# A softmax kernel: one scaled row in eight on ScalarE, and the last four rows of two tiles loaded in DMAs of chosen partition counts

## The chip, the cores and the metric

The kernel runs on one core of a Trainium2 chip. The metric is the device time of one execution in microseconds (us). HBM is the large memory that holds x and the result, SBUF the memory beside the engines, with 128 partitions (rows). A DMA is a transfer between the two; 16 DMA engines carry it out in packets, and each engine ends its part with a semaphore write of 4 bytes, which marks its data as landed (before the change the packet records hold 160 for the ten loads and 128 for the eight stores, 16 each). The median before the change is 162.49 us (2 runs, 162.41 to 162.57). Apart from one experiment, which is marked, all runs were in the fast state. Times "in the span" count from the start of the profiled span, which is about 1.8 us shorter than the device time.

## The reference

```python
x = randn(16, 1024, 512)            # float32, 32 MiB
x_scaled = x / 0.5
exp_x = exp(x_scaled - max(x_scaled, axis=-1))
out = exp_x / sum(exp_x, axis=-1)   # float32, 32 MiB
```

This is a softmax over rows of 512. Every byte is read once and written once: 33.55 MB in, 33.55 MB out.

## The kernel before

The 16,384 rows form eight tiles of 128 partitions x 16 rows x 512 elements (4 MiB, 32 KiB in each partition, contiguous in HBM). SP issues the loads, ACT (ScalarE) the stores. VectorE (DVE) finds the maxima, ScalarE does the exponentials with their sums. The scaling by 1/sum is divided: VectorE takes three rows in four, ScalarE one in four. The kernel keeps six tiles in SBUF, so load 6 must wait for store 0 and load 7 for store 1.

```python
LOADS = [[(0, 1), (1, 4), (4, G)]] + [WHOLE] * 7          # G = 16 rows
BLOCKS = [[(0, 4), (4, 8), (8, G)]] + [WHOLE] * 6 + [[(0, 8), (8, G)]]
...
def load(c):
    ...
    for lo, hi in LOADS[c]:
        nc.sync.dma_start(out=xt[:, lo:hi, :], in_=xr[c][:, lo:hi, :])
...
def scale_vector(i):
    ...
    k = b - b // 4
    ...                              # DVE: rows 0..k of the block times recip
def scale_scalar(i):
    for g in range(b - b // 4, b):
        ...                          # ACT: one copy with a scale per row
...
for i in range(n):
    if i + 1 < n:
        exponentials(i + 1)
    scale_vector(i)
    scale_scalar(i)
    if i + 2 < n:
        shift(i + 2)                 # loads its tile, then maxima on DVE
    store(i)
```

## Time and profile before

| | before |
|---|---|
| device time, median | 162.49 us |
| DVE busy, ACT busy | 125.6 us (78%), 112.5 us (70%) |
| DMA engines: the two data queues, share of the 16 engines' span | 49.3% + 48.4% |
| one 32 KiB packet, load or store (packet records of the trace) | 1.213 us, so 27.0 GB/s per engine |
| last store issued | 140.3 us |
| store 6 landed on the 16 engines | 148.6 to 149.5 us |
| last store landed | 158.3 to 159.2 us |

The first lines are from the page of the kernel before: busy time by engine, then the span in 40 slices (each digit is the busy share in tenths) with the rate in GB/s, the two data queues (q1 carries the loads, q10 the stores), two groups (busy us, mean ns, idle time before them and its cause), and the issues of whole tiles with their median time to landing.

```profile
...
DVE 125.6 (78%) x45; ACT 112.5 (70%) x290; POOL 0.2 (0%) x4
...
DVE  0507999999999999999999999999799994800000
ACT  3071759089989989995999599959998969600000
...
DMA  5999999999999999999999999999999999999993
GB/s 169 477 398 465 449 392 465 449 392 443 465 392 392 400 392 498 416 392 473 441 394 457 449 400 441 465 400 432 473 400 416 481 400 416 489 400 408 498 400 139
...
q1 hardware_dynamic: 1440, 33.56, 49.3%
q10 hardware_dynamic: 1152, 33.55, 48.4%
q14 instruction: 3, 0.02, 0.0%
...
L74 DVE TENSOR_REDUCE negmax<-xt 128x16 f32<-128x8192 f32 (+2 forms) x11 | 69.9, 6353 | 10.7 <-DMA xt<-in_x_dram 10.7
L102 DVE TENSOR_TENSOR xt<-xt,recip 128x6144 f32<-128x6144 f32 (+2 forms) x11 | 52.9, 4813 | 0.4
...
out_dram<-xt ACTq DMA_DIRECT2D x8, 4096.0 KB, 24.8
xt<-in_x_dram SPq DMA_DIRECT2D x7, 4096.0 KB, 29.8
...
```

All DMA slices but the first and last read 9, and the two queues together fill 97.7% of the engines' span. VectorE also reads 9 in most slices from the fifth to the 33rd, but it has finished after slice 35, while DMA goes on to the end. The timeline of the kernel before shows the last store's issue (start, duration, engine):

```profile
...
140.32 0.34 ACTq L119 DMA_DIRECT2D out_dram<-xt  x1
```

At 140.3 us the engines still have 8 to 9 us of store 6 ahead of them, and then they need about 9.7 us for the last store (eight packets of 1.213 us each; store 7 lands 9.7 us after store 6 in the table). From an issue to its first packet some 1 us passes (0.73 to 1.72 us for the first load). Compute is therefore about 7 us early at the tail, and the kernel is bounded by the bytes of each DMA engine.

### The profile page before, as it was taken

What the parts mean: (1) busy time and instruction counts of PE and PEld (TensorE: products, weight loads), DVE (VectorE), ACT (ScalarE), POOL (GpSimd) and SP (SyncE); (2) the same over time, 40 slices, a digit from 0 to 9 for tenths busy, and PEclk for the clock granted to TensorE, in tenths of its full rate; (3) what the DMA queues carried; (4) which work ended last, traced back from release to release, by engine and by line L of the source; (5) the groups of instructions that cost most, each with busy time, mean ns of one, the idle gap of its engine ahead of it and who ended that gap; (6) DMA issues with size and microseconds to landing.
All of it is one profiled execution on the core that took longest, in us unless ns stands there. A gap on an engine that the chain in (4) does not pass through costs nothing.

```text
span 160.7 us, 421 instructions
## 1 busy us (share of the span) xinstructions
DVE 125.6 (78%) x45; ACT 112.5 (70%) x290; POOL 0.2 (0%) x4
## 2 busy tenths in 40 slices
DVE  0507999999999999999999999999799994800000
ACT  3071759089989989995999599959998969600000
POOL 0000000000000000000000000000000000000000
DMA  5999999999999999999999999999999999999993
GB/s 169 477 398 465 449 392 465 449 392 443 465 392 392 400 392 498 416 392 473 441 394 457 449 400 441 465 400 432 473 400 416 481 400 416 489 400 408 498 400 139
DMA packets 2595, 67.13 MB, mean 418 GB/s; under 512 B 289, under 2 KB 289, under 8 KB 545
## 3 DMA queue, kind: packets, MB, share of 16 engines
q1 hardware_dynamic: 1440, 33.56, 49.3%
q10 hardware_dynamic: 1152, 33.55, 48.4%
q14 instruction: 3, 0.02, 0.0%
HBM read 33.55 MB, written 33.55 MB: 418 GB/s over the span
## 4 chain that ended last, share of the span: by engine, by line
DMA 41%; DVE 24%; ACT 19%; issue 1%; SPq 1%; ACTq 0%
DMA xt<-in_x_dram 23%; DMA out_dram<-xt 18%; ACT xt L85 17%; DVE negmax L74 15%; DVE xt L102 8%; ACT xt L111 2%; DVE bias L78 1%; SPq L66 1%; DVE recip L100 0%; ACTq L119 0%; ACTq L85 0%
## 5 line engine op out<-in xcount | busy, mean ns | idle before, releaser
L85 ACT ACTIVATE xt<-xt,bias 128x512 f32<-128x512 f32 x128 | 90.4, 707 | 25.8 <-DVE bias L78 24.8
L74 DVE TENSOR_REDUCE negmax<-xt 128x16 f32<-128x8192 f32 (+2 forms) x11 | 69.9, 6353 | 10.7 <-DMA xt<-in_x_dram 10.7
L102 DVE TENSOR_TENSOR xt<-xt,recip 128x6144 f32<-128x6144 f32 (+2 forms) x11 | 52.9, 4813 | 0.4
L85 ACT ACTIVATION_READ_ACCUMULATOR xt<-xt,bias 128x1 f32 x128 | 23.9, 187 | 0.0
L111 ACT ACTIVATE xt<-xt,recip 128x512 f32<-128x512 f32 x32 | 20.5, 706 | 0.0
L100 DVE RECIPROCAL recip<-sums 128x16 f32<-128x16 f32 (+2 forms) x11 | 2.4, 218 | 2.3 <-ACT xt L85 2.3
L78 DVE TENSOR_SCALAR bias<-negmax 128x16 f32<-128x16 f32 (+2 forms) x11 | 1.9, 173 | 0.4
L52 ACT ACT_TABLE_LOAD x1 | 1.3, 1283 | 0.7 <-PEq L148 0.7
L51 DVE MEMSET warm<- 128x1 f32 x1 | 0.1, 59 | 0.8 <-PEq L148 0.8
L52 ACT ACTIVATE warm<-warm 128x1 f32<-128x1 f32 x1 | 0.2, 203 | 0.0
L148 POOL MEMSET const-bfloat16-1.0<- 128x1 bf16 x1 | 0.1, 102 | 0.0
L148 POOL MEMSET const-uint8-127<- 128x1 uint8 x1 | 0.1, 102 | 0.0
L148 POOL MEMSET const-float32-0.0<- 128x1 f32 x1 | 0.1, 99 | 0.2 <-issue 0.2
L148 POOL MEMSET const-float32-1.0<- 128x1 f32 x1 | 0.1, 99 | 0.0
## 6 DMA issues: line engine op xcount, KB each, us to landing
out_dram<-xt ACTq DMA_DIRECT2D x8, 4096.0 KB, 24.8
xt<-in_x_dram SPq DMA_DIRECT2D x7, 4096.0 KB, 29.8
xt<-in_x_dram SPq DMA_DIRECT2D x1, 3072.0 KB, 11.3
xt<-in_x_dram SPq DMA_DIRECT2D x1, 768.0 KB, 4.5
xt<-in_x_dram SPq DMA_DIRECT2D x1, 256.0 KB, 2.8
```

The lines of the kernel that those rows point to most:

```text
L51: nc.vector.memset(warm, 0.0)
L52: nc.scalar.activation(out=warm, in_=warm, func=EXP)
L66: nc.sync.dma_start(out=xt[:, lo:hi, :], in_=xr[c][:, lo:hi, :])
L74: nc.vector.tensor_reduce(negmax[:, 0:b], chunks[c][:, lo:hi, :], axis=AX, op=MAX, negate=True)
L78: nc.vector.tensor_scalar_mul(biases[i][:, 0:b], negmax[:, 0:b], 2.0)
L85: nc.scalar.activation(out=row, in_=row, func=EXP, bias=biases[i][:, g : g + 1], scale=2.0, accum_out=sums[i][:, g : g + 1],)
L100: nc.vector.reciprocal(recips[i][:, 0:b], sums[i][:, 0:b])
L102: nc.vector.tensor_mul(rows, rows, recips[i][:, 0:k].unsqueeze(2).broadcast_to((P, k, D)))
L111: nc.scalar.activation(out=row, in_=row, func=COPY, scale=recips[i][:, g : g + 1])
L148: nc = _bacc.Bacc("TRN2", target_bir_lowering=False, num_devices=1)
```

## The change

The intent is to move scaling work from ScalarE to VectorE, to simplify the first load, and to load the last four rows of tiles 1 and 2 in DMAs of 2, 6, 10, 14, 96 and 4, 8, 8, 12, 96 partitions. The counts were meant to give different DMA engines different numbers of packets, so that they can be told apart.

```diff
-    LOADS = [[(0, 1), (1, 4), (4, G)]] + [WHOLE] * 7
+    LOADS = [[(0, 4), (4, G)]] + [WHOLE] * 7
 ...
+        if c in SPLITS:
+            load_split(c)
+            return
 ...
+    SPLITS = {1: [2, 6, 10, 14, 96], 2: [4, 8, 8, 12, 96]}
+    LAST = slice(G - 4, G)
+
+    def load_split(c):
+        nc.sync.dma_start(
+            out=chunks[c][:, 0 : G - 4, :], in_=xr[c][:, 0 : G - 4, :]
+        )
+        p = 0
+        for k in SPLITS[c]:
+            nc.sync.dma_start(
+                out=chunks[c][p : p + k, LAST, :], in_=xr[c][p : p + k, LAST, :]
+            )
+            p += k
+        assert p == P
 ...
-        k = b - b // 4
+        k = b - b // 8
 ...
-        for g in range(b - b // 4, b):
+        for g in range(b - b // 8, b):
```

## The prediction

> **What bounds the kernel now: the 16 DMA engines, each by its own bytes.** The page's slices show DMA at 9 in 38 of 40 (queues: 49.3% + 48.4% of the engines' span). The packet records are sharper: a 32 KiB packet takes 1.213 us, load or store (27.0 GB/s per engine); packets sum to 156.8 us per engine, between the first at 1.72 us and the last landing at 159.2 us of a 160.7 us span. DVE is 78% busy, ACT 70%. The last store is issued at 140.3 us (timeline) but store 6 lands only at 148.6 to 149.5 us, so compute has about 7 us of slack at the tail.
>
> **What the change does**
>
> 1. Scale split. DVE multiplies 7/8 instead of 3/4 of the rows: 128x6144 takes 6.56 us, 128x3072 3.36 us, so 128x7168 about 7.65 and 128x3584 about 3.92 (estimates by line): +9.3 us over 11 blocks, about 135 us busy. ACT loses 16 copies of 0.706 us (112.5 to about 101). DVE is gapless from 13 to 114 us, so all shifts: the last tile's reductions start near 120.8 us instead of 114.9 (the 1.1 us wait for that load vanishes). The last store goes out near 148 us, not 140.3. This eats nearly all the slack, but hardly more: first packets can run at about 149.1 us (the first load took 1.0 us from issue to packet), against 148.6 to 149.5 us when the engines finished store 6 before.
>
> 2. First load in two DMAs instead of three. Tile 0 lands at about 12.4 us, while its 256 KiB per engine at 27.0 GB/s from 1.72 us would be 11.4. About 0.2 us may be regained.
>
> 3. Marked loads. [...] Before, the last store's landings spread from 158.3 to 158.8, with one engine at 159.2: an average engine plus 1.2 us is only 0.6 us later than the old last one. The 24+8 KiB packets cost perhaps 0.1 us over 32 KiB ones. Eight more issues of about 0.4 us on SP are far ahead of need.
>
> **Sum**: +1.2 (marks) -0.5 (the old laggard is probably another engine) +0.1 (small packets) -0.2 (start) = +0.6 us. Predicted 163.1 us, range 162.3 to 164.5. Faster by over 2%: 0.01; within 2%: 0.95; slower by over 2%: 0.04.
>
> **Shown right by**: busy DVE near 135 us; last multiply ending near 148 us; DMA slices still 9 to the end[...].
>
> **Wrong if**: the last store needs far longer from issue to first packet (store 0, issued to a busy engine at 45.2 us, had its first packet at 49.5): then +2 to +4 us[...].

Statements of how the chip divides a load among its engines, which no run had shown, are cut from the prediction, and the cuts are marked. The sum: +1.2 - 0.5 + 0.1 - 0.2 = +0.6 us on 162.49 us, so 163.1 us. Its first term: the author assumed that the marked loads would give two engines 32 KiB more than the average, and 32 KiB at the measured 27.0 GB/s are 1.21 us. So the term is the author's estimate (e16 tests a surplus of that size).

## The result, and the profile after

The changed kernel takes 170.31 us (median of 2 runs, 170.12 to 170.50), 1.0468 times the time before, with a 95% interval of 1.043 to 1.0507. A ratio is the mean time of one kernel's fast runs over that of the other's fast runs of the same rounds, so it is not quite the ratio of the medians quoted. The prediction was 163.1 us with a range up to 164.5, so the result is far outside.

The same lines from the page of the changed kernel:

```profile
...
DVE 135.0 (80%) x45; ACT 102.1 (61%) x273; POOL 0.2 (0%) x4
...
DVE  0508988997999999999999999499974999959000
ACT  3063366079959954995599459940999393392000
...
DMA  5999999999999999999999999999999999995893
GB/s 197 438 455 450 311 271 420 290 276 366 436 436 428 428 444 420 452 405 467 397 452 420 452 422 436 436 428 436 405 444 420 452 413 459 413 444 226 382 491 132
...
q1 hardware_dynamic: 1648, 33.56, 50.5%
q10 hardware_dynamic: 1152, 33.55, 46.3%
q14 instruction: 2, 0.02, 0.0%
...
L93 DVE TENSOR_REDUCE negmax<-xt 128x16 f32<-128x8192 f32 (+2 forms) x11 | 69.9, 6356 | 17.3 <-DMA xt<-in_x_dram 17.3
L121 DVE TENSOR_TENSOR xt<-xt,recip 128x7168 f32<-128x7168 f32 (+2 forms) x11 | 62.0, 5637 | 0.4
...
out_dram<-xt ACTq DMA_DIRECT2D x8, 4096.0 KB, 22.4
xt<-in_x_dram SPq DMA_DIRECT2D x5, 4096.0 KB, 29.3
...
```

The compute groups are as predicted: DVE is busy for 135.0 us. The DMA row still reads 9 in slices 4 to 9 (counted from 0), yet the rate below it falls from about 430 to between 271 and 311 GB/s in four of them. The engines are not idle there; they are slow. This shows more sharply in the windows view, which gives busy time by engine, clock, DMA share and rate for a stretch of time; the loads of the last four rows of tile 1 fill the stretch from 20 to 24 us of the changed kernel. (The view counts a short stretch coarsely: a share can exceed 1, and stretches with equally fast packets can differ in rate, as 393 GB/s here and 475 GB/s in e3 below.) First before, then after:

```profile
...
20.00:24.00 4.00, 3.93 (x5) 2.08 (x6) 0.00 (x0) 1.00 0.91 393
...
```

```profile
...
20.00:24.00 4.00, 3.93 (x4) 1.55 (x5) 0.00 (x0) 1.00 1.10 248
...
```

The packet records say which packets are slow. The 8 KiB packets of tile 0's first load, 128 partitions at once, mostly take 0.309 us. The 256 packets of 8 KiB in the marked loads have a median of 0.581 us and reach 0.796 us.

The timeline of the changed kernel has the last store at 155.7 us instead of 140.3:

```profile
...
155.68 0.34 ACTq L138 DMA_DIRECT2D out_dram<-xt  x1
```

The chain of waits of the changed kernel (start, duration, what) shows where that lateness comes from. Load 7 lands only at 128.65 us, then the maxima, exponentials and multiplies of the last tile follow:

```profile
...
90.18 38.47 DMA xt<-in_x_dram
...
128.67 4.43 DVE negmax L93
...
145.68 5.76 ACT xt L104 x16
...
151.70 3.89 DVE xt L121
```

Landings of the 16 engines, sorted, in us of the span, worked out from the semaphore writes among the packet records:

```
load 7, before   112.3 112.3 112.4 112.4 ... 112.8 113.9 113.9 113.9 114.5
load 7, after    120.2 120.2 120.6 120.8 ... 124.9 125.1 126.0 128.3
store 6, before  148.6 148.6 148.7 148.8 ... 149.0 149.0 149.2 149.5
store 6, after   152.9 152.9 153.2 153.3 ... 155.2 155.4 156.3 157.4
store 7, before  158.3 158.3 158.4 158.4 ... 158.7 158.7 158.8 159.2
store 7, after   166.3 166.3 166.3 166.3 ... 166.4 166.4 166.4 167.1
```

Two limits meet at the end. The slowest engine ends store 6 at 157.4 us and needs 9.7 us more, which gives the 167.1 us seen. The other 15 run dry, wait for the late store and land together at 166.3 to 166.4. Even the fastest engine is 4 us later than before at store 6, so there is a loss common to all engines and an unevenness on top of it.

One detail of the division was checked in these records. The load queue has 240 semaphore writes. Eleven loads of 128 or 96 partitions at 16 each, plus 2+6+10+14+4+8+8+12 = 64, give exactly 240, so the small loads together ended with one write per partition. The pages of e9 and e16 below agree: their load queues have 1568 and 1480 packets against 1440 before, which is 64 data packets and 64 writes for eight loads of 8 partitions, and 20 and 20 for loads of 2, 4, 6 and 8. Which engines took the small loads, the records do not name.

### The profile page after: what moved, and what is told of

The parts are those of the page before. It is cut to its first block, busy times and chain, and to the rows that moved or that the text cites. A ratio compares the mean times of both kernels' runs of the same rounds, so it can differ in the third digit from the quotient of the medians.

```text
span 168.3 us, 422 instructions
## 1 busy us (share of the span) xinstructions
DVE 135.0 (80%) x45; ACT 102.1 (61%) x273; POOL 0.2 (0%) x4
## 4 chain that ended last, share of the span: by engine, by line
DMA 62%; DVE 18%; ACT 10%; SPq 1%; issue 1%; DVEq 0%; ACTq 0%
DMA xt<-in_x_dram 45%; DMA out_dram<-xt 17%; DVE negmax L93 10%; ACT xt L104 10%; DVE xt L121 7%; ACT xt L130 1%; SPq L81 1%; SPq L69 0%; DVE bias L97 0%; SPq L76 0%; DVE recip L119 0%; DVEq L93 0%; ACTq L104 0%
## 5 line engine op out<-in xcount | busy, mean ns | idle before, releaser
L121 DVE TENSOR_TENSOR xt<-xt,recip 128x7168 f32<-128x7168 f32 (+2 forms) x11 | 62.0, 5637 | 0.4
L130 ACT ACTIVATE xt<-xt,recip 128x512 f32<-128x512 f32 x15 | 9.9, 705 | 0.0
```

The costliest lines, as they stand in the source:

```text
L121: nc.vector.tensor_mul(rows, rows, recips[i][:, 0:k].unsqueeze(2).broadcast_to((P, k, D)))
L130: nc.scalar.activation(out=row, in_=row, func=COPY, scale=recips[i][:, g : g + 1])
```

## The theories

**P, partitions.** The packets of a load of fewer than 128 partitions can be slow, and how slow depends on which partitions it writes. The changed kernel's 0.581 us beside 0.309 us suggested about 0.6 us for such loads. The expectations call what slows them a collision. Which partitions collide and by how much, and so the other figures of P, rested on a supposition that no run shows; it is cut from the expectations, with the cuts marked. The prediction did not consider this.

**D, compute.** VectorE's extra work made the last store late.

**S, a cost per DMA.** Every DMA costs each engine that takes part a fixed time at its end. To explain the loss it would have to be about 0.56 us: the slowest engine ended 7.9 us later, 1.2 of them are its surplus of bytes, and an engine that takes part in every load of tiles 1 and 2 ends 12. The 1.2 us are the estimate named beside the prediction. The expectations below use 0.57.

**I, unequal bytes.** The surplus of the most loaded engines is worth more than the 1.2 us predicted.

**H, HBM.** The addresses read at one time collide in HBM.

## The experiments

Unless told otherwise, a kernel is the kernel before with one edit, and its result is correct. "Phase" is the time from the first start to the last end of the 8 KiB packets of one tile's last four rows (1 MiB), from the packet records. The profile lines shown are of the windows view unless another is named.

| run | loads of the last four rows of tiles 1 and 2, or other edit | time, us (before beside it) | ratio | median 8 KiB packet, us | phase of tiles 1, 2, us |
|---|---|---|---|---|---|
| the change | 2, 6, 10, 14, 96 and 4, 8, 8, 12, 96 | 170.31 (162.49) | 1.047 | 0.581 | 5.7, 7.7 |
| e1_marks_only | the same, scale split as before | 170.12 (162.64) | 1.046 | 0.588 | |
| e2_split_only | whole tile | 162.46 (162.64) | 1.000 | | |
| e3_no_marks | 128 | 162.41 (162.64) | 0.999 | 0.309 | 2.8, 2.9 |
| e4_halves | 64, 64 | 167.97 (162.64) | 1.033 | 0.609 | 5.3, 5.5 |
| e5_sixteens | eight of 16 neighbours | 171.44 (162.54) | 1.054 | 0.834 | 7.5, 7.5 |
| e8_sixteens_step4 | eight of 16, four apart | 167.82 (162.54) | 1.032 | 0.585 | 4.8, 4.9 |
| e6_six_full | whole tile in six loads of 128 | 163.05 (162.54) | 1.002 | | |
| e7_96_32 | 96, 32 | 166.73 (162.54) | 1.027 | 0.512 | 4.5, 4.6 |
| e11_all_vector | no scaling on ScalarE | 168.86 (162.48) | 1.039 | | |
| e16_marks_home | extra loads, 2, 4, 6, 8 partitions four apart | 164.25 (162.58) | 1.010 | 0.309 | |

### e1_marks_only, e2_split_only: which part of the change

e1 is the kernel before with `load_split` and `SPLITS` of the change; e2 is the kernel before with this edit:

```diff
-        k = b - b // 4
+        k = b - b // 8
-        for g in range(b - b // 4, b):
+        for g in range(b - b // 8, b):
```

> The kernel before with the marked loads alone (scale split and first load as before). Theory P [...]: nearly the whole loss is here, 169.5 to 170.5 us, last store landings spread over 4 to 5 us. Rival D (VectorE's extra 9.3 us made the last store late): 163 to 163.8 us, only the 1.2 us of imbalance.

> The kernel before with one row in eight on ScalarE and nothing else. P: the 7 us of slack take it up, 162.3 to 163.3 us, last multiply ending near 148 us. D: 166 us or more.

e1 has the whole loss (ratio 1.0459, interval 1.0428 to 1.0491) and e2 none (0.9997, 0.9974 to 1.0021). D falls. The timeline of e2 has the last store at 147.6 us:

```profile
...
147.63 0.34 ACTq L119 DMA_DIRECT2D out_dram<-xt  x1
```

It still lands at 158.2 to 159.1 us, as before. So the slack of 7 us was read correctly. In e1, the timeline shows the last store at 151.9 us, nearly 4 us earlier than in the changed kernel, and the time is nevertheless the same:

```profile
...
151.91 0.34 ACTq L137 DMA_DIRECT2D out_dram<-xt  x1
```

There store 7 lands between 162.6 and 166.4 us, spread by its engines. The late last store of the changed kernel is a consequence that runs beside the slowest engine, and does not add to it.

### e3_no_marks and e4_halves: small packets, or few partitions

e3 is the changed kernel with one 128-partition DMA in place of five; e4 is the kernel before with two of 64.

```diff
-    SPLITS = {1: [2, 6, 10, 14, 96], 2: [4, 8, 8, 12, 96]}
+    SPLITS = {1: [128], 2: [128]}          # e3
+    SPLITS = {1: [64, 64], 2: [64, 64]}    # e4
```

> The changed kernel with the last four rows of tiles 1 and 2 in one DMA of 128 partitions each instead of five. P: 162 to 163.2 us, 8 KiB packets at about 310 ns. If small packets as such, or the extra 24 KiB plus 8 KiB cut, were the cause: 166 us or more, packets near 600 ns.

> The kernel before with the last four rows of tiles 1 and 2 in two DMAs of 64 partitions each[...]. P: [...] these 2 MiB take twice as long, about 600 ns a packet and +2.4 us per tile: 167.0 to 167.8 us. Rival S (each DMA costs every engine that takes part a fixed time at its end, 0.57 us if it is to explain the loss): four more DMAs, 164.8 us, packets at 310 ns. Rival I (only unequal bytes matter): 162.5 us.

e3 is as fast as the kernel before (0.9993, 0.9971 to 1.0014), with 8 KiB packets of 0.309 us. Neither the cut of 24 KiB plus 8 KiB nor the first load in two pieces matters to the time. e4 loses 3.3% (1.0312 to 1.0349). Its 167.97 us is just above what P said (167.0 to 167.8) and far from S (164.8) and I (162.5). How many bytes each engine got is not in the records, but the phases bound it (an estimate): 5.3 and 5.5 us hold at most nine packets of 0.609 us, where an equal share is eight, so a surplus could be one packet in each tile, 1.2 us of the 5.3 us lost. Unequal bytes alone fall as the cause. First e3, then e4:

```profile
...
20.00:24.00 4.00, 3.93 (x4) 1.85 (x5) 0.00 (x0) 1.00 1.11 475
...
```

```profile
...
20.00:24.00 4.00, 3.60 (x4) 2.17 (x7) 0.00 (x0) 1.00 1.13 254
...
```

The DMA share is full in both, and the rate of e4 is about half. The packets of e4 take 0.609 us, twice 0.309. The phases are longer than e3's by 2.5 and 2.6 us, which is 5.1 us of the 5.3 us lost.

### e5_sixteens and e8_sixteens_step4: the same reads, other partitions

e5 has `SPLITS = {1: [16] * 8, 2: [16] * 8}`. e8 reads the same rows of HBM in the same order, into partitions four apart (so its rows are permuted and its result is wrong):

```diff
-        for k in SPLITS[c]:
+        for m in range(8):
+            h, j = m // 4, m % 4
+            p = 64 * h + j
             nc.sync.dma_start(
-                out=chunks[c][p : p + k, LAST, :], in_=xr[c][p : p + k, LAST, :]
+                out=chunks[c][p : p + 61 : 4, LAST, :],
+                in_=xr[c][16 * m : 16 * m + 16, LAST, :],
             )
```

> The kernel before with the last four rows of tiles 1 and 2 in eight DMAs of 16 neighbouring partitions each[...]. P: [...] packets take about 1.2 us, the 1 MiB takes 9.9 instead of 2.5 us, +14.8 us in all: 177 us. S (0.57 us per DMA and engine): 16 x 0.57 = 9.1, 171.7 us with packets of 310 ns. Rival H (the HBM addresses read at one time collide): slow too, no size given.

> As e5_sixteens, same eight DMAs reading the same rows of HBM in the same order, but each writes 16 partitions four apart instead of neighbours (the result is wrong on purpose, rows are permuted). P: [...] packets near 600 ns, +5 us in all: 167.6 us. S: equal to e5_sixteens. H: equal to e5_sixteens, as HBM sees the same reads.

e5 measured 171.44 us, which misses P's 177 us and hits S's 171.7. The number alone would have favoured the wrong theory. The packets decide: S had them at 0.310 us, and they take 0.893 us in tile 1 and 0.828 us in tile 2. e8, which differs from e5 only in the partitions written, has 0.585 us and 167.82 us, as P said. H and S both required e8 to equal e5. So the partitions written decide between 0.834 and 0.585 us. That the rest, from 0.309 to 0.585 us, is also a matter of the partitions written is not shown: P had foretold about 0.6 us for it, but from the changed kernel's own packets, and no run makes these reads in DMAs of 16 at full speed. First e5, then e8:

```profile
...
20.00:24.00 4.00, 3.56 (x4) 2.21 (x7) 0.00 (x0) 1.00 1.04 148
...
```

```profile
...
20.00:24.00 4.00, 3.56 (x4) 2.21 (x7) 0.00 (x0) 1.00 1.13 283
...
```

P's figure for e5 was four times 0.309 us, 1.24 us. The factor of four was supposition and did not come: the packets took 2.9 times 0.309 us in tile 1 and 2.7 times in tile 2. Why, the runs do not show.

### e6_six_full and e7_96_32: number of DMAs, and another division

```diff
-    LOADS = [[(0, 1), (1, 4), (4, G)]] + [WHOLE] * 7
+    LOADS = (                                          # e6
+        [[(0, 1), (1, 4), (4, G)]]
+        + [[(0, 6), (6, 8), (8, 10), (10, 12), (12, 14), (14, G)]] * 2
+        + [WHOLE] * 5
+    )
+    SPLITS = {1: [96, 32], 2: [96, 32]}                # e7, with load_split
```

> The kernel before with tiles 1 and 2 each loaded in six DMAs of 128 partitions (6, 2, 2, 2, 2, 2 rows), so as many DMAs per tile as the changed kernel has and packets of 4 and 12 KiB. P: [...] 162.3 to 162.9 us. S: 10 more DMAs x 0.57 = +5.7, 168 us.

> The kernel before with the last four rows of tiles 1 and 2 in two DMAs of 96 and 32 partitions[...]. P: [...] +2.5 us in all, 165.0 us. S and H have no reason to differ from e4_halves: 167.9 us.

e6 loads tiles 1 and 2 in as many DMAs as the changed kernel and is 0.2% slower (0.9999 to 1.0049, two runs, so not clear of noise), not 5.7 us: S falls. e7, with as many DMAs as e4, lies below it as P said (1.0274, 1.0229 to 1.0319, against 1.033), with faster packets (0.512 us) and shorter phases. But at 166.73 us it is above P's 165.0. The author's count behind that figure, which no run shows, gives the right order and too small a loss for this shape.

### e9 to e15: attempts to separate unequal bytes from collisions

These kernels add extra loads into a spare tile that nobody reads. The "home" ones use 8 partitions four apart (0, 4, ..., 28), which by supposition do not collide; the "near" ones use 8 neighbours. The estimates in the expectations take it that the same eight engines carry all extra loads of a run, 64 KiB each in e9 to e13 and 56 KiB in e14 and e15; the two groups of eight in e12 bear this out.

```diff
+    spare = stats.tile([P, 4, D], fp32, name="spare", bufs=1)
 ...
+        if c == 1:                        # e9 and e10; behind tile 1's load
+            for h in range(2):
+                for j in range(4):
+                    p = 32 * h + j        # e9;  e10: p = 32 * h + 8 * j
+                    nc.sync.dma_start(    # e10: spare[p : p + 8], same rows of xr
+                        out=spare[p : p + 29 : 4], in_=xr[c][p : p + 29 : 4, 0:4, :]
+                    )
```

e12 and e13 put four of these loads behind tile 1 and four behind tile 2 (`if c in (1, 2)`). e14 and e15 put four of them, with rows of 14 KiB, behind tile 5 (`if c == 5`).

> The kernel before plus eight extra loads behind tile 1's, each of 8 partitions four apart (0, 4, ... 28 and so on) with 8 KiB rows, into a spare tile that nobody reads. [...] P with imbalance: packets about 310 ns, the loaded engines end 2.43 us later (64 KiB at 27.0 GB/s): 164.9 us, last store landings in two groups about 2.4 us apart. If engines could share the work: 163.7 us. S (0.57 us per DMA and engine): +4.6, 167 us.

e9 took 166.16 us (1.0226). Its packets were at 0.309 us, as P wanted, but all engines ended late alike, not in two groups. The windows view tells why:

```profile
...
22.00:24.00 2.00, 2.00 (x2) 2.00 (x7) 0.00 (x0) 1.00 0.50 205
...
```

Half of the engines are idle: SP issued tile 2's load only at 23.3 us, because it waited for an earlier load. The timeline shows SP's issue of the extra loads stretching over 20.68 us, and then the next tile:

```profile
...
2.58 20.68 SPq L72 DMA_DIRECT2D spare<-in_x_dram  x8
...
23.30 1.97 SPq L67 DMA_DIRECT2D xt<-in_x_dram  x4
...
```

So this run does not measure what it was made for. The changed kernel also shows SP waiting at its marked loads, but its DMA share stays at 1 or above in the window shown, so there the waiting costs nothing.

> As e9_extra_home, same count, bytes and engines, but each extra load writes 8 neighbouring partitions[...]. P: [...] packets of 0.85 to 1.24 us (0.89 was the median in e5_sixteens), so the eight engines end 7 to 10 us later: 169.5 to 172.5 us. Imbalance alone or S: equal to e9_extra_home.

e10: two fast runs are at 167.7 us (ratio 1.0317), two slow ones at 170.6 us, and the profiled one is slow. It lies above e9; it starves engines like e9, so no more is drawn from it.

> e9_extra_home with four of its extra loads behind tile 1 and four behind tile 2, so that SP, which here never has more than eight loads out, is not kept from issuing the next tile (in e9_extra_home eight engines sat idle for over 2 us for that reason). [...] Unequal bytes cost one for one: packets of 310 ns, last store landings in two groups of eight about 2.4 us apart, 164.9 us (+1.5%). If the engines even out: one group, 163.7 us.

That SP has at most eight loads out fits the trace of the changed kernel: SP issued eight by 4.2 us, the ninth at 5.70 us, after the first had landed at 5.35 us, and the tenth at 12.97 us, after the second had landed at 12.62 us.

> The same bytes, counts and engines as e12_extra_home_spread, but each extra load writes 8 neighbouring partitions [...]. P: packets about 0.8 us as in e10_extra_near, so the eight engines end 8 x (0.8 - 0.31) = 3.9 us later still: 168.8 us[...]. Bytes alone: equal to e12_extra_home_spread.

e12 took 167.11 us (1.0264) and e13 170.48 us (1.0481). In e12 the engines do fall into two groups of eight (load 3 landed at 41.3 to 41.7 and at 43.6 to 44.5 us), some 2.2 us apart where 2.4 us were expected. But the end is set by something else: load 5 waited until store 0 had landed, and was issued at 64.7 us, where the kernel before has it out before 5 us. That is SP's first issue after 60 us in the timeline of e12:

```profile
...
64.72 1.49 SPq L67 DMA_DIRECT2D xt<-in_x_dram  x2
...
```

The extra loads had changed which completions SP waits for. Both kernels end on a late last store, and e13 is 2% above e12 with equal bytes and counts, which agrees with P but is not a clean measure. The packets are one: all 64 extra packets of e12 took 0.309 us, and the 64 of e13, with the same sizes and counts, have a median of 0.648 us and reach 0.924 us.

> In e12 the engines fell into two groups 2.3 us apart as expected, but load 5 went out only when store 0 had landed, the queues ran dry and all ended together; so the end showed nothing. Here the extra loads stand behind load 5, where the issue of tiles 0 to 5 is untouched: four loads of 8 partitions four apart, 14 KiB rows[...]. Unequal bytes cost one for one: 56 KiB at 27.0 GB/s = +2.1 us, 164.7 us (+1.3%), last store landings in two groups of eight 2.1 us apart.

> e14 with 8 neighbouring partitions in each extra load: same bytes, counts, engines, issue times. P: 14 KiB packets at about 2.5 times their free time (e10: 0.79 against 0.31 us), so the eight engines lose another 3.3 us: 168 us, groups of landings further apart. Bytes alone: equal to e14.

e14 took 165.23 us (1.0158; 164.7 expected) and e15 166.07 us (1.0194; 168 expected). The time of e14 is near the one expected, but by luck. In neither are there groups at the end: the last store came at 151.7 us and all 16 engines of e14 landed it at 162.3 to 162.5 us. The reason is instructive. The records fit loads and stores that alternate on each engine by packet, so each extra 14 KiB packet held up the load queue by itself and by the store packets between. There are two of these, because the semaphore write of each load takes a turn of its own (the first packet ended at 75.34 us, its semaphore write began at 76.54 us, one store packet later): successive extra packets start 2.96 us apart, which is 0.535 + 2 x 1.213, and the last 1.75 us, which is 0.535 + 1.213. So 2.1 us of bytes (four packets of 0.535 us) put load 7 of the loaded engines up to 13.3 us behind that of the fastest (125.9 against 112.6 us). In e15 the median packet took 0.536 us, as if free; 13 of the 32 took 0.60 to 0.99 us. Summed over the packets, that is 0.4 us more for each of the eight engines, where P said 3.3 us, so a near load costs little there. Why, the runs do not show.

### e11_all_vector: how much slack there is

```diff
-        k = b - b // 4
+        k = b
-        for g in range(b - b // 4, b):
+        for g in range(b, b):
```

> The kernel before with no scaling on ScalarE at all, to test the reading of 7 us slack at the tail. e2_split_only issued its last store at 147.6 us and lost nothing. Here VectorE's chain is about 7.6 us longer again, the last store goes out near 155 us, the DMA engines run dry before it, and the end follows: 168.5 to 170 us. If VectorE has more slack than I think: 163 us.

It took 168.86 us, inside the range expected. The timeline shows the last store at 155.2 us, and all engines landed it together at 165.8 to 166.0:

```profile
...
155.22 0.34 ACTq L119 DMA_DIRECT2D out_dram<-xt  x1
```

With e2 this brackets the slack: 147.6 us costs nothing, 155.2 us costs 3.9%.

### e16_marks_home: the marks' surplus in partitions four apart

```diff
+        if c == 1:
+            for j, k in enumerate((2, 4, 6, 8)):
+                end = j + 4 * k - 3
+                nc.sync.dma_start(
+                    out=spare[j:end:4], in_=xr[c][j:end:4, 0:4, :]
+                )
```

> The kernel before plus marks of the same surplus as the changed kernel's[...]: behind tile 1 four extra loads of 2, 4, 6 and 8 partitions that lie four apart, 8 KiB rows, into a spare tile. [...] If unequal bytes are a small matter and collisions the cause: packets of 310 ns, +1.2 us at most, 162.7 to 163.9 us. If unequal bytes, by way of the late last load, explain most of the 8 us: 166 us or more.

It costs 1.0% (1.0084 to 1.0116), 1.6 us, with 8 KiB packets of 0.309 us throughout. The median of 164.25 us is a little above the 163.9 us allowed, and far below 166. The landings of the last store form a ladder:

```
store 7, e16  158.4 158.5 158.5 158.5 158.6 158.6 158.7 158.7 158.7 159.1 159.1 159.1 159.3 159.4 159.7 160.5
```

Its top is 1.3 us above the 159.2 us of the kernel before. If the four loads share engines, so that two engines carry all four, two carry three, two carry two and two carry one, the surpluses at 27.0 GB/s are 1.2, 0.9, 0.6 and 0.3 us (an estimate). Above the 158.5 us of most others this gives steps of 159.7, 159.4, 159.1 and 158.8 us, two engines each, and with 159.2 us as the old laggard's base a top of 160.4 us. The ladder fits this within some 0.3 us; the records do not name the engines.

## Why the prediction was wrong

1. **The bound, right.** The DMA engines bound the kernel, each by its own bytes. e2 moved 9 us of work to VectorE and changed nothing.
2. **The scale split, right.** DVE is busy 135.0 us, the multiplies take 7.625 and 3.891 us, and in e2 the last store is issued at 147.6 us, where 148 was predicted. The 7 us of slack are confirmed by e2 and e11.
3. **The first load, too small to tell.** The prediction hoped for 0.2 us. e3, which has the two-piece load, and e2, which has not, are at 162.41 and 162.46 us.
4. **The marks as bytes, right within 0.4 us.** The surplus of 32 KiB was put at +1.2 us. e16, with that surplus by the estimate beside its ladder and packets of 0.309 us, costs 1.6 us. The discount of 0.5 us for an old laggard on another engine did not come.
5. **The marks as packets, wrong.** The step that failed is "The 24+8 KiB packets cost perhaps 0.1 us over 32 KiB ones". It took a packet's time from its size alone. By size it holds: the changed kernel's packets have medians of 0.912 us (24 KiB) and 0.309 us (8 KiB, tile 0), 1.221 us against 1.213, or 0.13 us over 16 pairs. But the marked loads do not run at that rate. The term of +0.1 us stands for what the runs put at some 6 us (an estimate: 7.8 us lost, less the 1.6 us of point 4). In the marked loads a packet takes 0.581 us instead of 0.309 us. The phases of tiles 1 and 2 last 5.7 and 7.7 us, where e3 needs 2.8 and 2.9. The difference is about 7.8 us, and so is the loss of the kernel; it includes what the unequal bytes cost in these phases. The packet records of the two traces agree as an average over the engines: the data packets sum to 156.8 us per engine before and to 162.6 us after.
6. **The end, wrong in consequence.** "DMA slices still 9 to the end" did not come: slices 36 and 37 read 5 and 8. The landings of the last store lie within 0.8 us. The backlog doubled on the way: tile 2's landings are 3.7 us apart (35.3 to 39.0 us), load 7's 8.1 us, which fits a load queue that gets only every other packet while stores run (before the change whole loads land 9.7 us apart until the stores begin, tiles 1 and 2, and 19.4 us apart beside them, tiles 5 and 6). Load 7 was late, so the last store was late, and 15 engines ran dry. e1 shows that this did not add to the time.

The loss of 4.7% divides, by subtraction and so as an estimate, into about 1.0% for unequal bytes (e16), nothing for the scale split and the first load (e2, e3), and the rest, some 3.7%, for the slow packets of the marked loads. That the partitions written set the duration of a packet is shown by e5 and e8 (0.834 and 0.585 us), which make the same reads; e3 and e6 rule out the packet size and the number of DMAs, and in e12 and e16 DMAs of 2 to 8 partitions run their packets in 0.309 us, so few partitions as such are not slow. For the counts of the change itself the cause is carried over from these runs: its packets take 0.581 us, beside 0.609 us in e4 and 0.585 us in e8. By what mechanism the partitions written slow a packet, the runs do not show. No version found here beats both kernels: e2 and e3 are equal to the kernel before within 0.3%.

## What to carry to other kernels

Load a tile in DMAs of all 128 partitions and cut it by rows, not by partitions: loading two tiles in six DMAs of 128 each cost at most 0.5%, loading a quarter of each in two DMAs of 64 cost 3.3%. If a DMA must have few partitions, try them four apart instead of neighbours (a packet took 0.309 us in e12 and 0.648 us in e13 with 8 partitions, 0.585 us in e8 and 0.834 us in e5 with 16), and look at the duration of a packet as well as at the busy share, because an engine with slow packets counts as fully busy (a share of 1.13 at 254 GB/s in e4). And when a surplus is put into one of two alternating queues, watch what waits for the last transfer of that queue, since its delay can be larger than the surplus (up to 13.3 us for 2.1 us in e14).
